# A decoder step on one core: the first tile of the out projection is multiplied in another order, and the last normalization is spread in pieces over three engines and two DMA queues

## The chip, the cores and the metric

The kernel runs on one core of one Trainium2 chip. The metric is the device time of one execution in microseconds. One execution has been profiled; its span runs from the first to the last instruction.

## The reference, cut to what matters

The reference is one inference step of a small hybrid decoder over 544 tokens: a prompt of 512 and 8 samples of 4. The first layer is a state space mixer, the second attends over dilated windows, and a final norm ends the trunk:

```
u = rmsnorm(h, g_norm) @ w_in                       # 1024 -> 5152: z, x|B|C, dt
...                                                 # convolution, SSD scan -> y (l, 2048)
y = rmsnorm(y * silu(z), g_gate)                    # z: the last column tiles of w_in to be computed
h = h + y @ w_out                                   # "out projection", 2048 -> 1024
...                                                 # shared K/V, dilated window attention
h = h + y_att @ b_w_out                             # 1024 -> 1024
y_out = h * rsqrt(mean(h * h) + eps) * final_norm   # over the 1024 features of a token
```

All arrays are float32.

## The kernel before, in words

Features lie on the 128 partitions and tokens in the free dimension. A projection is computed in tiles of 128 output features. For each there are two PSUM buffers: `pa` for the first 256 tokens and `pb` for the other 288. Three PSUM buffers of this kind take turns.

Every product is made of three fast ones. A weight is split into a high part (`whi`, rounded, by ScalarE, L199) and a low part (`wlo`, the remainder, by VectorE, L200), an activation likewise. Per slice of 128 input features TensorE multiplies high by high, high by low and low by high (`proj_steps`, called through `full`). `load_w` fetches a weight of eight slices into one of three `wraw` buffers, on SyncE's DMA queue, and splits it; `whi` and `wlo` have two buffers each.

The first stage ends with ten tiles of z (`z_tile` in `filler_a`). Their order is a list, and each weight is fetched and split while the tile ahead of it is multiplied. The gated result `v` (four groups of four slices) is split by `v_split` into `vh` and `vl` (L757 on ScalarE, L758 on VectorE): groups 0 and 1 within the z tiles, 2 and 3 behind them. The sum of squares `ssq` is collected on GpSimd (L598).

The out projection has 16 input slices, so each of its tiles has two weights: slices 0 to 7 and 8 to 15 (`load_out`). In the first tile, `m == 0`, the slices are multiplied in an order of their own: 0 to 11 into `pa`, 0 to 11 into `pb`, 12 to 14 into both, the mean square `ms` of the gated result, then slice 15. The later tiles go straight through.

The kernel is recorded in a framework that schedules it: the order of the instructions on each engine comes from the program's order, from priorities (`high_priority` around the splits) and from what each instruction waits for. Matmuls of the second layer and of its out projection (`out_proj`) are made in a fixed order.

At the end `out_proj` adds the last product to the residual for two parts of the tokens, 272 each. Part 0 is normalized while part 1 is multiplied. For part 1 everything behind the last product is in the open: `norm_sum` (the squares summed over features, into PSUM `ms`), `rstd_fin` (ScalarE's square root, VectorE's reciprocal, L267, three scalings of an identity into `dgs`, L270, and one product with ones that spreads the factors over all partitions, `rp` in PSUM), then `norm_mul` with four multiplies on VectorE (L1456), two feature tiles at a time, each followed by a DMA to the output on SyncE's queue (L1457). `dgs`, `tmps` and `accs` are pieces of one SBUF tile `e`, and appear as `e` in the rows.

Of the kernel before, what the change touches and what calls it, by code (L numbers as in the profile page):

```python
# [12 lines left out]
F32 = mybir.dt.float32  # L13
F32R = mybir.dt.float32r
AF = mybir.ActivationFunctionType
ALU = mybir.AluOpType
# [7 lines left out]
T = SEQ + NB * TS  # L24
HA = 256
HB = T - HA
KD = D // 128
# [97 lines left out]
def tile_yoco_step(  # L125
# [6 lines left out]
    nc = tc.nc  # L132
    dma = nc.sync.dma_start
    pinned = [False]

    def pin(ins):
        if pinned[0]:
            tc.keep_in_program_order(ins)
# [3 lines left out]
    def mm(*a, **k):  # L142
        pin(nc.tensor.matmul(*a, **k))  # L143
# [4 lines left out]
    const = ctx.enter_context(tc.tile_pool(name="const", bufs=1))  # L148
# [8 lines left out]
    def pj(name, cols=512):  # L157
        return psum.tile([128, cols], F32, name=name, tag="pj", bufs=3)

    def pss(name, shape=(128, 512)):  # L160
        return psum.tile(list(shape), F32, name=name, tag="ss", bufs=5)
# [10 lines left out]
    ident = const.tile([128, 128], F32, name="ident")  # L172
    make_identity(nc, ident)
    ones = const.tile([128, 128], F32, name="ones")
# [5 lines left out]
    epst = const.tile([128, 1], F32, name="epst")  # L180
# [7 lines left out]
    def fetch_w(src):  # L188
        raw = wpool.tile([128, 8, 128], F32, name="wraw", bufs=3)
        dma(raw, src)  # L190
        return raw

    def split_w(raw, both=None, lo_eng=nc.vector, fixed=False):
        if both is None:
            hi = wpool.tile([128, 8, 128], F32R, name="whi", bufs=2)
            lo = wpool.tile([128, 8, 128], F32R, name="wlo", bufs=2)
        else:
            hi, lo = both[:, 0], both[:, 1]
        a = nc.scalar.activation(hi, raw, AF.Copy)  # L199
        b = lo_eng.tensor_tensor(lo, raw, f32(hi), op=ALU.subtract)  # L200
        if fixed:
            hold(a)
            hold(b)
        return hi, lo

    def load_w(src, both=None, lo_eng=nc.vector):
        raw = fetch_w(src)
        with tc.high_priority():
            return split_w(raw, both, lo_eng)
# [10 lines left out]
    def proj_steps(p, ws, act_h, act_l, c0, c1, k0=0, k1=None, order=None):  # L220
        n = len(ws) * 8
        o = p[:, 0:c1 - c0]
        order = order or range(n)
        for i in range(k0, n if k1 is None else k1):
            k = order[i]
            hi, lo = ws[k // 8]
            ah, al = act_h[k // 4][:, k % 4, c0:c1], act_l[k // 4][:, k % 4, c0:c1]
            mm(o, hi[:, k % 8, :], ah, start=i == 0, stop=False)
            yield
            mm(o, hi[:, k % 8, :], al, start=False, stop=False)  # L230
            yield
            mm(o, lo[:, k % 8, :], ah, start=False, stop=i == n - 1)
            yield

    def full(*a, **k):
        for _ in proj_steps(*a, **k):
            pass
# [147 lines left out]
    for i in range(2):  # L385
        sq, xa = sqx[i][:, :, 0:HA], x_t[i][:, :, 0:HA]
        n = 4 - 2 * i
# [6 lines left out]
    hi = wpool.tile([128, 8, 128], F32R, name="whi", bufs=2)  # L394
    lo = wpool.tile([128, 8, 128], F32R, name="wlo", bufs=2)
# [34 lines left out]
    for i in range(3):  # L430
        cbs.append(conv_in(first[i], pp[i]))
        pb = pj("pb")
# [7 lines left out]
    dgs = tm[:, 1200:1584].rearrange("p (a b) -> p a b", b=128)  # L440
# [312 lines left out]
    def v_split(g, i):  # L753
        gg = g_gate[:, 4 * g + i:4 * g + i + 1]
        if i == 0:
            v_h[g], v_l[g] = half("vh", F32R), half("vl", F32R)
        nc.scalar.activation(v_h[g][:, i, :], v_t[g][:, i, :], AF.Copy, scale=gg)  # L757
        nc.vector.scalar_tensor_tensor(v_l[g][:, i, :], v_t[g][:, i, :], gg, f32(v_h[g][:, i, :]),  # L758
                                       op0=ALU.mult, op1=ALU.subtract)

    v_h, v_l = [None] * 4, [None] * 4

    def filler_a():
        nxt = load_w(w_in[5])
        for i, (kind, t) in enumerate(IN_ORDER):
            if i < 5:
                continue
            w = nxt
            if i + 1 < len(IN_ORDER):
                nxt = load_w(w_in[i + 1])  # L770
            yield from (conv_tile if kind == "x" else z_tile)(t, w)
            if kind == "x" and t == 3:
                yield from tok_transposes()
            if kind == "z" and t in (13, 14):
                for j in range(4):
                    v_split(t - 13, j)
# [12 lines left out]
    for c0, c1 in ((0, HA), (HA, T)):  # L789
        for i in range(2):  # L790
            p = pj("pa")
# [34 lines left out]
    ms = pss("ms")  # L826
# [35 lines left out]
        (nc.gpsimd if m < KD - 1 else nc.vector).tensor_tensor(hss, hss, sq, op=ALU.add)  # L862

    def load_out(m):
        return [load_w(w_out[m, :, 0:8, :]), load_w(w_out[m, :, 8:16, :])]

    def bias_tables():
        rl = wk.tile([66, 384], F32, name="rl", tag="tv", bufs=2)
# [53 lines left out]
    for m in range(KD):  # L922
        w = nxt
        pa, pb = pj("pa"), pj("pb")
        if m == 0:
            full(pa, w, v_h, v_l, 0, HA, 0, 12)
            full(pb, w, v_h, v_l, HA, T, 0, 12)
            full(pa, w, v_h, v_l, 0, HA, 12, 15)
            full(pb, w, v_h, v_l, HA, T, 12, 15)
            ms_add(ms, ssq, inv_i, True, True)  # L930
            full(pa, w, v_h, v_l, 0, HA, 15)
            full(pb, w, v_h, v_l, HA, T, 15)
            nxt = load_out(1)
            prev = pa, pb
            continue
        if m == 1:
            full(pa, w, v_h, v_l, 0, HA, 0, 5)
            rs_v = rstd_of(ms)
            h1_tile(0, *prev)
            full(pa, w, v_h, v_l, 0, HA, 5)  # L940
        else:
            full(pa, w, v_h, v_l, 0, HA)
        if m + 1 < KD:
            nxt = load_out(m + 1)
        full(pb, w, v_h, v_l, HA, T)
        h1_tile(m, pa, pb)
        next(tables, 0)
# [30 lines left out]
    for i, (f, h, wi) in enumerate(order):  # L978
        w = [nxt]
        pa, pb = pj("pa"), pj("pb")  # L980
        if i == 0:
# [4 lines left out]
            ms = pss("ms")  # L986
# [35 lines left out]
    for k in range(4):  # L1022
        b1, b2 = (wk.tile([128, T], F32, name="hb", bufs=2) for _ in range(2))
# [33 lines left out]
    scale = 1.0 / math.sqrt(128.0)  # L1057
# [370 lines left out]
    def out_proj():  # L1428
        h2 = [half("h2"), half("h2")]
        for i in range(2):  # L1430
            dma(h2[i], h1d[:, 4 * i:4 * i + 4, :])
        e = half("e").rearrange("p a b -> p (a b)")
        accs, tmps = [e[:, HB * i:HB * i + HB] for i in range(2)], [e[:, HB * (2 + i):HB * (3 + i)] for i in range(2)]
        dgs = [e[:, HB * (4 + i):HB * (5 + i)] for i in range(2)]
        wos = {}

        def get(m):
            if m < KD and m not in wos:
                wos[m] = load_w(wo[m], half("wo", F32R, (128, 2, 8, 128)) if m < KD - 2 else None)

        def norm_sum(part, c0, c1):
            n = c1 - c0
            b0s = (0, 128, n - 128) if n > 256 else (0, 128)
            ms = pss("ms")
            for s_ in (0, 1):
                for b, b0 in enumerate(b0s):
                    mm(ms[:, b:b + 1], (accs, tmps)[s_][part if s_ == 0 else 1][:, b0:b0 + 128], inv_d,
                       start=s_ == 0 and b == 0, stop=s_ == 1, skip_group_check=True)
            return ms, n, b0s

        def norm_mul(sums, part, c0, c1):
            ms, n, b0s = sums
            rs = rstd_fin(ms, n, b0s, dgs[part])
            for m in range(0, KD, 2):
                hm = h2[m // 4][:, m % 4:m % 4 + 2, c0:c1]
                nc.vector.tensor_tensor(hm, hm, rs[:, None, 0:n].to_broadcast([128, 2, n]), op=ALU.mult)  # L1456
                dma(yT[:, m:m + 2, c0:c1], hm)  # L1457

        get(0)
        parts = ((TH, T), (0, TH))  # L1460
        for part, (c0, c1) in enumerate(parts):
            n = c1 - c0
            acc = accs[part]
            for m in range(KD):
                get(m + 1)
                p = pj("pa")
                yield from proj_steps(p, [wos[m]], y_h, y_l, c0, c1, order=(0, 1, 2, 3, 5, 7, 6, 4))
                if part and m == 0:
                    sums = norm_sum(0, *parts[0])
                if part and m == 1:  # L1470
                    norm_mul(sums, 0, *parts[0])
                hm = h2[m // 4][:, m % 4, c0:c1]
                sq = acc if m == 0 else tmps[m % 2]
                nc.vector.tensor_tensor(hm, p[:, 0:n], hm, op=ALU.add)
                nc.scalar.activation(sq[:, 0:n], hm, AF.Square)
                if 0 < m < KD - 1:
                    nc.gpsimd.tensor_tensor(acc[:, 0:n], acc[:, 0:n], sq[:, 0:n], op=ALU.add)
                nc.scalar.activation(hm, hm, AF.Copy, scale=g_f[:, m:m + 1])
        norm_mul(norm_sum(1, *parts[1]), 1, *parts[1])

    ahead = [0]

# [129 lines left out]
```

## Time and profile before

| | |
|---|---|
| three runs | 945.29 us median, 944.85 to 950.9 |
| profiled execution | 946.21 us |
| its span | 944.4 us, 21805 instructions |
| TensorE busy | 916.7 us, 97% |
| VectorE, ScalarE, GpSimd busy | 682.1, 478.7, 200.5 us |
| mean granted TensorE clock | 0.991 |

PE is TensorE's matmuls, PEld its weight loads, DVE is VectorE, ACT ScalarE, POOL GpSimd, and SPq and ACTq are the DMA issues of SyncE and ScalarE. A row of the order of time gives the start, the length, the engine, the line, the operation, what is written from what, and in square brackets the idle time ahead of it with what ended it. A product of two plain float32 tiles, such as `ms`, `rp` or `idle`, is two matmul records. A row of the waits gives the total, the number and the longest. A row of a stretch gives its length, then the busy time and the instructions of PE, PEld, DVE, ACT and POOL, the granted clock, the DMA share and GB/s.

### The profile page before, as it was taken

How to read it: one execution, taken by the hardware profiler on the slowest of the kernel's cores; microseconds unless marked ns; L12 is line 12 of the kernel's file. 1: busy time of each engine (PE TensorE's matmuls, PEld its weight loads, DVE VectorE, ACT ScalarE, POOL GpSimd, SP SyncE). 2: the span in 40 equal slices, each digit the busy share in tenths (PEclk: the TensorE clock that was granted, in tenths of full speed). 3: DMA queues.
4: the chain of work that ended last, by engine and by line, in shares of the span. 5: the costliest groups of instructions: out<-in, count | busy, mean ns of one | idle time of the engine just before them, and what ended most of it. 6: DMA issues, size and time to landing. Idle time of an engine off the chain costs nothing.

```text
span 944.4 us, 21805 instructions
## 1 busy us (share of the span) xinstructions
PE 916.7 (97%) x8645; PEld 844.0 (89%) x8645; DVE 682.1 (72%) x1423; ACT 478.7 (51%) x1069; POOL 200.5 (21%) x295
## 2 busy tenths in 40 slices
PE   7999999899999998999999999999999999999996
PEld 5999888789788888999999999988888988888996
DVE  6688988997997889544589435876677766778632
ACT  5558744655556644322245213555555555557642
POOL 2232644733725642111101000000000000000021
PEclk9999999899999999999999999999999999999998
DMA  7252255254454452436377555757767767785411
GB/s 261 87 141 92 101 198 189 81 201 142 157 179 154 167 177 100 147 102 216 102 240 233 178 191 197 267 174 263 247 201 259 272 203 259 262 249 192 158 44 52
DMA packets 75934, 168.49 MB, mean 178 GB/s; under 512 B 19446, under 2 KB 37192, under 8 KB 75320
## 3 DMA queue, kind: packets, MB, share of 16 engines
q1 hardware_dynamic: 71880, 154.91, 50.1%
q10 hardware_dynamic: 2880, 9.44, 2.6%
q0 software_dynamic: 1072, 2.74, 1.1%
q8 instruction: 68, 1.11, 0.5%
q14 instruction: 34, 0.28, 0.1%
HBM read 141.14 MB, written 25.93 MB: 177 GB/s over the span
## 4 chain that ended last, share of the span: by engine, by line
PE 85%; DVE 6%; DMA 5%; ACT 2%; POOL 1%; issue 1%; DVEq 0%; SPq 0%; ACTq 0%
PE pa L143 34%; PE pb L143 29%; PE sp L143 3%; PE pv L143 2%; PE so L143 2%; PE s L143 2%; DMA m<-aed 2%; DMA kc<-ck 1%; PE yd L143 1%; PE csp L143 1%; PE w L146 1%; PE ptp L146 1%; PE yo L143 1%; PE xp L146 1%; PE yos L143 1%
## 5 line engine op out<-in xcount | busy, mean ns | idle before, releaser
L199 ACT ACTIVATE whi<-wraw 128x1024 fp32r<-128x1024 f32 x72 | 76.1, 1057 | 99.2 <-PE pb L143 64.7
L200 DVE TENSOR_TENSOR wlo<-wraw,whi 128x1024 fp32r<-128x1024 f32 x71 | 88.8, 1251 | 51.6 <-ACT whi L199 51.3
L143 PE MATMUL pa<-bq,whi 128*128 128x272 f32 x512 | 103.1, 296 | 0.0
L143 PE MATMUL pa<-xh,whi 128*128 128x256 f32 (+1 forms) x320 | 92.7, 293 | 3.3 <-ACT xh L365 3.3
L143 PE MATMUL pb<-xh,whi 128*128 128x288 f32 (+1 forms) x304 | 90.4, 299 | 3.9 <-ACT cb L331 3.9
L143 PE MATMUL pb<-xl,whi 128*128 128x288 f32 (+1 forms) x304 | 91.3, 302 | 0.9 <-DVE xl L368 0.8
L143 PE MATMUL pa<-xl,whi 128*128 128x256 f32 (+1 forms) x320 | 90.8, 287 | 0.9 <-DVE xl L368 0.8
L143 PE MATMUL pb<-xh,wlo 128*128 128x288 f32 (+1 forms) x304 | 87.4, 299 | 0.0
L143 PE MATMUL pa<-xh,wlo 128*128 128x256 f32 (+1 forms) x320 | 85.0, 283 | 0.0
L143 PEld LDWEIGHTS pa<-bq,whi 128*128 128x128 f32 x512 | 81.2, 189 | 0.9
L143 PE MATMUL pb<-bq,whi 128*128 128x272 f32 x384 | 77.2, 296 | 0.5 <-DVE kv L1103 0.5
L143 PE MATMUL pa<-bq,wlo 128*128 128x272 f32 x256 | 74.1, 290 | 0.0
L529 DVE SCALAR_TENSOR_TENSOR co<-cb,cvp,co 128x568 f32<-128x568 f32 x72 | 66.3, 921 | 1.2 <-ACT co L527 0.2
L143 PEld LDWEIGHTS pa<-xh,whi 128*128 128x128 f32 x320 | 60.7, 190 | 6.2 <-ACT xh L365 3.7
L143 PEld LDWEIGHTS pa<-xl,whi 128*128 128x128 f32 x320 | 60.7, 190 | 3.4 <-DVE xl L368 1.4
L143 PEld LDWEIGHTS pb<-xl,whi 128*128 128x128 f32 x304 | 57.8, 190 | 6.5 <-issue 4.4
L143 PEld LDWEIGHTS pb<-xh,whi 128*128 128x128 f32 x304 | 58.0, 191 | 5.0 <-ACT cb L331 4.1
L143 PEld LDWEIGHTS pb<-bq,whi 128*128 128x128 f32 x384 | 60.8, 189 | 1.8 <-DVE kv L1103 0.8
L1339 POOL COPY lse<-mxs 128x1 f32<-128x1 f32 x16 | 4.6, 289 | 267.7 <-DVE mxs L1337 267.7
L143 PEld LDWEIGHTS pa<-xh,wlo 128*128 128x128 f32 x320 | 58.0, 188 | 1.2 <-issue 0.9
L1162 ACT ACTIVATE whi<-wraw 128x512 fp32r<-128x512 f32 x64 | 40.1, 627 | 37.1 <-PE pa L143 17.5
L143 PEld LDWEIGHTS pb<-xh,wlo 128*128 128x128 f32 x304 | 56.6, 190 | 2.2 <-issue 2.2
(379 smaller groups left out, 2771.4 us busy)
## 6 DMA issues: line engine op xcount, KB each, us to landing
wraw<-w_in SPq DMA_DIRECT2D x40, 512.0 KB
kc<-ck SPq DMA_DIRECT2D x32, 640.0 KB
vc<-cv SPq DMA_DIRECT2D x32, 640.0 KB
wraw<-wb SPq DMA_DIRECT2D x32, 512.0 KB
s<-s SPq DMA_DIRECT2D x16, 512.0 KB
m<-aed SPq DMA_DIRECT2D x16, 512.0 KB
ssmS<-s ACTq DMA_DIRECT2D x16, 512.0 KB
wraw<-w_out SPq DMA_DIRECT2D x16, 512.0 KB
```

What stands on the lines that cost most here:

```text
L143: pin(nc.tensor.matmul(*a, **k))
L146: pin(nc.tensor.transpose(*a))
L199: a = nc.scalar.activation(hi, raw, AF.Copy)
L200: b = lo_eng.tensor_tensor(lo, raw, f32(hi), op=ALU.subtract)
L529: nc.vector.scalar_tensor_tensor(o, cb[:, k:k + n], cvp[:, ti, k:k + 1], o, op0=ALU.mult, op1=ALU.add)
L1162: nc.scalar.activation(hi, src[p][j], AF.Copy)
L1339: nc.gpsimd.tensor_copy(lse[:, i16:i16 + 1], mx[:, 2:3])
```

## The change

The first weight of the out projection is fetched and split by the last round of `filler_a` (before: by `load_out`, called behind it). In the tile `m == 0` slices 0 to 7 go into `pa` and then into `pb`, in each with all products of the high weight ahead of those of the low one; slices 8 to 11 follow for both.

The end gets a function of its own, `norm_last`. The scalings of the identity are shared between ScalarE (its middle piece) and VectorE. Six products of ones by ones stand ahead of the spread, and their result is not used. The spread is made in two pieces, 128 and 144 wide. ScalarE copies it to SBUF. GpSimd multiplies the last two feature tiles with the copy, and ScalarE's queue writes them; VectorE multiplies the other six from PSUM, and SyncE's queue writes these.

```
+    out_first = []
...
+            else:
+                out_first.append(load_w(w_out[0, :, 0:8, :]))
...
-        return [load_w(w_out[m, :, 0:8, :]), load_w(w_out[m, :, 8:16, :])]
+        return [load_w(w_out[m, :, 0:8, :]) if m else out_first[0], load_w(w_out[m, :, 8:16, :])]
...
         if m == 0:
-            full(pa, w, v_h, v_l, 0, HA, 0, 12)
-            full(pb, w, v_h, v_l, HA, T, 0, 12)
+            for p, c0, c1 in ((pa, 0, HA), (pb, HA, T)):
+                hi, lo = w[0]
+                for k in range(8):
+                    mm(p[:, 0:c1 - c0], hi[:, k, :], v_h[k // 4][:, k % 4, c0:c1], start=k == 0, stop=False)
+                    mm(p[:, 0:c1 - c0], hi[:, k, :], v_l[k // 4][:, k % 4, c0:c1], start=False, stop=False)
+                for k in range(8):
+                    mm(p[:, 0:c1 - c0], lo[:, k, :], v_h[k // 4][:, k % 4, c0:c1], start=False, stop=False)
+            full(pa, w, v_h, v_l, 0, HA, 8, 12)
+            full(pb, w, v_h, v_l, HA, T, 8, 12)
...
+        def norm_last(sums, part, c0, c1):
+            ms, n, b0s = sums
+            sd = const.tile([128, 5], F32, name="sd", bufs=2)
+            nc.scalar.activation(sd[:, 0:3], ms[:, 0:3], AF.Sqrt, bias=epst)
+            nc.vector.reciprocal(sd[:, 0:3], sd[:, 0:3])
+            idle = pss("idle")
+            for _ in range(6):
+                mm(idle[:, 0:128], ones, ones, start=True, stop=True)
+            dg, rp = dgs[part], pss("rp")
+            nc.scalar.activation(dg[:, 128:256], ident, AF.Copy, scale=sd[:, 1:2])
+            nc.vector.tensor_scalar(dg[:, 0:128], ident, sd[:, 0:1], None, op0=ALU.mult)
+            nc.vector.tensor_scalar(dg[:, 256:n], ident[:, 384 - n:128], sd[:, 2:3], None, op0=ALU.mult)
+            for b0, b1 in ((0, 128), (128, n)):
+                mm(rp[:, b0:b1], ones, dg[:, b0:b1], start=True, stop=True, skip_group_check=True)
+            rs = tmps[0][:, 0:n]
+            nc.scalar.copy(rs, rp[:, 0:n])
+            for m in range(KD - 2, KD):
+                hm = h2[m // 4][:, m % 4, c0:c1]
+                nc.gpsimd.tensor_tensor(hm, hm, rs, op=ALU.mult)
+                nc.scalar.dma_start(yT[:, m, c0:c1], hm)
+            for m in range(0, KD - 2, 2):
+                hm = h2[m // 4][:, m % 4:m % 4 + 2, c0:c1]
+                nc.vector.tensor_tensor(hm, hm, rp[:, None, 0:n].to_broadcast([128, 2, n]), op=ALU.mult)
+                dma(yT[:, m:m + 2, c0:c1], hm)
...
-        norm_mul(norm_sum(1, *parts[1]), 1, *parts[1])
+        norm_last(norm_sum(1, *parts[1]), 1, *parts[1])
```

What this does to the order on the engines is seen at three places. The first is VectorE at the change from the z tiles to the out projection: `pa` and `pb` are those of the last z tiles, the first `L200` splits slices 0 to 7 of the out projection's first weight, the second slices 8 to 15. Before:

```order
L592 TENSOR_TENSOR v<-v,uz 128x544
L200 TENSOR_TENSOR wlo<-wraw,whi 128x1024
L565 SCALAR_TENSOR_TENSOR uz<-zth,pb 128x288
L592 TENSOR_TENSOR v<-v,uz 128x544
L565 SCALAR_TENSOR_TENSOR uz<-zth,pa 128x256
L592 TENSOR_TENSOR v<-v,uz 128x544
L758 SCALAR_TENSOR_TENSOR vl<-v,gn,vh 128x544 x4
L200 TENSOR_TENSOR wlo<-wraw,whi 128x1024
L565 SCALAR_TENSOR_TENSOR uz<-zth,pb 128x288
```

After the change VectorE has the same rows in the same order here, and so have ScalarE, GpSimd and SyncE.

The second place is TensorE in the first tile of the out projection, where slice 7 ends and what follows begins. Before, the first and second weight half follow each other in `pa`, and `pb` comes behind slice 11:

```order
L143 MATMUL pa<-vh,whi 128x256
L143 MATMUL pa<-vl,whi 128x256
L143 MATMUL pa<-vh,wlo 128x256
L143 MATMUL pa<-vh,whi 128x256
L143 MATMUL pa<-vl,whi 128x256
L143 MATMUL pa<-vh,wlo 128x256
L143 MATMUL pb<-vh,whi 128x288
L143 MATMUL pb<-vl,whi 128x288
```

After, from slice 7 of `pa` to slice 0 of `pb`, and then, behind the dots, from slice 7 of `pb` to slice 8 of `pa`:

```order
L143 MATMUL pa<-vl,whi 128x256
L143 MATMUL pa<-vh,wlo 128x256 x8
L143 MATMUL pb<-vh,whi 128x288
L143 MATMUL pb<-vl,whi 128x288
...
L143 MATMUL pb<-vl,whi 128x288
L143 MATMUL pb<-vh,wlo 128x288 x8
L143 MATMUL pa<-vh,whi 128x256
L143 MATMUL pa<-vl,whi 128x256
L143 MATMUL pa<-vh,wlo 128x256
```

So 24 matmuls into `pb` have moved in between slices 7 and 8 of `pa`.

The third place is the end of the program, with what each instruction waits for. VectorE before:

```order
L270 TENSOR_SCALAR e<-ident,sd 128x128
L270 TENSOR_SCALAR e<-ident,sd 128x16
L1456 TENSOR_TENSOR h_11459<-h_11459,rp 128x2x272 [waits PE_49]
L1456 TENSOR_TENSOR h_11459<-h_11459,rp 128x2x272
L1456 TENSOR_TENSOR h_11460<-h_11460,rp 128x2x272 x2
```

VectorE after, then ScalarE after and TensorE after:

```order
L1481 TENSOR_SCALAR e<-ident,sd 128x128 [waits DVE_49]
L1482 TENSOR_SCALAR e<-ident,sd 128x16
L1493 TENSOR_TENSOR h_11459<-h_11459,rp 128x2x272 [waits Activation_49]
L1493 TENSOR_TENSOR h_11459<-h_11459,rp 128x2x272
L1493 TENSOR_TENSOR h_11460<-h_11460,rp 128x2x272
```

```order
L1515 ACTIVATE h_11460<-h_11460,gn 128x272 [waits Activation_49]
L1474 ACTIVATE sd<-ms,epst 128x3 [waits PE_49]
L1480 ACTIVATE e<-ident,sd 128x128 [waits DVE_49]
L1486 COPY e<-rp 128x272 [waits PE_49,Pool_49]
L1490 DMA yT<-h_11460 128x272 [waits Pool_49] x2
```

```order
L143 MATMUL ms<-inv,e 128x1 x2
L143 MATMUL idle<-ones 128x128 [waits PE_49]
L143 MATMUL idle<-ones 128x128 x5
L143 MATMUL rp<-e,ones 128x128 [waits DVE_49]
L143 MATMUL rp<-e,ones 128x144 [waits DVE_49,Activation_49]
```

VectorE's first multiply, which waited for TensorE, now waits for ScalarE, and the count that it waits for is that of the copy L1486. The spread stands behind the idle products in TensorE's queue.

## The prediction

> **What bounds the kernel now.** I read the page first, then the waits of the matrix engine, then the order of time around the two places that the change touches.
>
> ```profile
> PE 916.7 (97%) x8645; PEld 844.0 (89%) x8645; DVE 682.1 (72%) x1423; ACT 478.7 (51%) x1069; POOL 200.5 (21%) x295
> PE 85%; DVE 6%; DMA 5%; ACT 2%; POOL 1%; issue 1%; DVEq 0%; SPq 0%; ACTq 0%
> ```
>
> TensorE is busy for 916.7 of the span's 944.4 us and carries 85% of the chain that ended last. So an edit is worth something only where it removes a wait of TensorE or shortens the stretch behind its last matmul. There are 27.7 us of idle TensorE in all. The view of its waits says what ended them:
>
> ```profile
> PE pb L143 <- ACT cb L331: 3.9, 1, 3.9
> PE pa L143 <- ACT xh L365: 3.3, 1, 3.3
> PE pa L143 <- DVE wlo L200: 2.9, 1, 2.9
> PE s L143 <- DMA kc<-ck: 0.6, 2, 0.4
> ```
>
> The first two lie in the prologue, which the change leaves alone. The third is one wait of 2.9 us for the low part of a weight. The order of time puts it in the first tile of the out projection (TensorE, then VectorE):
>
> ```profile
> 369.85 0.28 PE L143 MATMUL pa<-vh,whi 128*128 128x256 f32 x1
> 372.80 0.28 PE L143 MATMUL pa<-vl,whi 128*128 128x256 f32 x1
> 375.93 0.38 PE L143 MATMUL pa<-vh,wlo 128*128 128x256 f32 x1 [2.86 <-DVE wlo L200]
> 376.15 0.28 PE L143 MATMUL pa<-vh,whi 128*128 128x256 f32 x1
> 377.22 0.29 PE L143 MATMUL pb<-vh,whi 128*128 128x288 f32 x1
> 382.02 0.28 PE L143 MATMUL pa<-vh,whi 128*128 128x256 f32 x1
> 365.46 1.22 DVE L200 TENSOR_TENSOR wlo<-wraw,whi 128x1024 fp32r<-128x1024 f32 x1
> 367.59 0.41 DVE L565 SCALAR_TENSOR_TENSOR uz<-zth,pa 128x256 f32<-128x256 f32 x1
> 368.56 6.18 DVE L758 SCALAR_TENSOR_TENSOR vl<-v,gn,vh 128x544 fp32r<-128x544 f32 x4
> 374.66 1.21 DVE L200 TENSOR_TENSOR wlo<-wraw,whi 128x1024 fp32r<-128x1024 f32 x1
> 376.16 0.77 DVE L758 SCALAR_TENSOR_TENSOR vl<-v,gn,vh 128x544 fp32r<-128x544 f32 x1
> 377.49 3.28 DVE L758 SCALAR_TENSOR_TENSOR vl<-v,gn,vh 128x544 fp32r<-128x544 f32 x3
> ```
>
> Slices 0 to 7 (first weight half) are 24 matmuls into pa, 369.85 to about 372.7. Slice 8 begins with the high part, and the matmul with the low part, due at 372.92, starts at 375.93. Note which weight is late. The split at 365.46 is that of the **first** half, done at 366.7, over 3 us before its use. The one at 374.66 is that of the **second** half. It stands in VectorE's queue behind the four splits of v that start at 368.56, and ends at 375.87.
>
> **The change at the out projection.** The words promise an earlier split. But VectorE's rows are the same before and after (the order shown above), and so are ScalarE's and SyncE's here: the split of the first half already stood in the last z tile. This edit by itself I cost at 0. Placing the low-part matmuls of a half behind its high ones gains nothing either, since that low part was ready at 366.7.
>
> What does count is that the first half is now multiplied into **both** pa and pb before the second half is touched. Pace in pa: 25 matmuls from 369.85 to 372.80, 0.118 each. Pace in pb: 36 from 377.22 to 382.02, 0.133 each. After the change: 24 into pa until 372.70, 24 into pb (3.20) until 375.90, two of slice 8, then its low part at 376.13. That weight is ready at 375.93, so the wait is gone, by a margin of 0.20. The new first wait of pb is for its buffer, last read by VectorE at 367.59 to 368.00: no cost.
>
> The number of matmuls is unchanged, so what is saved is the shift: 375.93 against the 372.92 at which that matmul was due, 3.01, and the 0.10 by which the restart exceeds the pace (0.22 from 375.93 to 376.15). Slice 12 starts at 378.92 in place of 382.02: **3.1 us**.
>
> What is late next? Slices 12 to 14 need the splits of v at 376.16 (done 376.93) and the first two of 377.49 (done by about 379), used at about 379.0, 379.4 and 379.7; the order of waits is one split per slice. The mean square needs GpSimd's last sum:
>
> ```profile
> 378.47 1.72 POOL L598 TENSOR_TENSOR ssq<-ssq,sq 128x544 f32<-128x544 f32 x1 [5.01 <-ACT sq L597]
> ```
>
> It ends at 380.19 and is now used at 381.2. Slice 15 follows the mean square, behind the last split (380.77). Nothing of this binds. Behind it TensorE has no gap that could swallow the gain:
>
> ```profile
> 386.00:480.00 94.00, 94.00 (x741) 93.27 (x740) 48.51 (x74) 27.41 (x34) 11.35 (x12) 1.00 0.47 147
> 480.00:565.00 85.00, 85.00 (x669) 83.84 (x669) 55.75 (x108) 32.85 (x71) 5.04 (x10) 1.00 0.65 215
> 565.00:700.00 135.00, 134.80 (x1508) 122.42 (x1507) 93.93 (x256) 66.05 (x164) 2.90 (x10) 1.00 0.69 227
> 700.00:845.00 145.00, 144.64 (x1870) 126.79 (x1868) 102.76 (x311) 79.17 (x214) 2.47 (x9) 1.00 0.75 245
> ```
>
> The first number behind the length is TensorE's busy time: 458.4 of 459 us. So I carry all of the 3.1 to the end. Its bounds are 0 (all given back) and 3.2 (the margin as well).
>
> **The change at the end.** The stretch behind the last product, then the output DMA by the microsecond (DMA share and GB/s stand last):
>
> ```profile
> 935.18 0.83 PE L143 MATMUL ms<-inv,e 128*128 128x1 f32 x6 [0.49 <-ACT e L1475]
> 936.04 0.26 ACT L266 ACTIVATE sd<-ms,epst 128x3 f32<-128x3 f32 x1 [0.36 <-PE ms L143]
> 936.34 0.17 DVE L267 RECIPROCAL sd<-sd 128x3 f32<-128x3 f32 x1 [1.74 <-ACT sd L266]
> 936.55 0.63 DVE L270 TENSOR_SCALAR e<-ident,sd 128x128 f32<-128x128 f32 x3
> 937.32 0.70 PE L143 MATMUL rp<-e,ones 128*128 128x272 f32 x2 [1.32 <-DVE e L270]
> 938.05 2.61 DVE L1456 TENSOR_TENSOR h<-h,rp 128x544 f32<-128x544 f32 x4 [0.88 <-PE rp L143]
> 938.85 2.25 SPq L1457 DMA_DIRECT2D yT<-h  x4
> 939.00:940.00 1.00, 0.00 (x0) 0.00 (x0) 1.00 (x3) 0.00 (x0) 0.00 (x0) 0.50 0.24 86
> 940.00:941.00 1.00, 0.00 (x0) 0.00 (x0) 0.67 (x2) 0.00 (x0) 0.00 (x0) 0.50 1.04 349
> 941.00:942.00 1.00, 0.00 (x0) 0.00 (x0) 0.00 (x0) 0.00 (x0) 0.00 (x0) 0.50 1.06 369
> 942.00:943.00 1.00, 0.00 (x0) 0.00 (x0) 0.00 (x0) 0.00 (x0) 0.00 (x0) 0.50 0.88 310
> ```
>
> The DMA engines begin at 939.76 (0.24 of that microsecond) and are full until 942.88, some 3.1 us for 1.11 MB; the span ends 1.5 us later. So the drain, and not VectorE's four multiplies, sets the end: only the time of the **first** write counts. I work that out.
>
> Six idle products are queued between the mean square and the spread, 12 records like those of yo, eight of which take 0.99:
>
> ```profile
> 337.01 1.05 PE L143 MATMUL yo<-CT,st 128*128 128x128 f32 x8
> 338.00 1.09 PE L143 MATMUL yd<-m,xdt 128*64 128x128 f32 x16
> ```
>
> That is 0.124 each. The six records of ms from 935.18 at that pace let them start at 935.93, and they hold TensorE until 937.42. Behind them wait the pieces of the spread, though their inputs are there by 937.0: one 128-wide scaling on VectorE and one on ScalarE side by side, each about 0.28, replace three in a row, a saving hidden entirely by the idle products. The two pieces are four records: 937.42 to about 938.08, against 938.02 before: +0.06.
>
> Then ScalarE copies the spread row to SBUF for GpSimd. In the order VectorE's first multiply no longer waits for TensorE but for ScalarE, so it is behind that copy. A 128x272 copy out of PSUM doesn't stand in the trace; the nearest row is
>
> ```profile
> L564 ACT ACTIVATE zth<-pb x14: 384/392/412, 133.0 to 370.9; 128x288 f32<-128x288 f32 x14
> ```
>
> so 0.39, plus 0.03 and 0.04 for the two hand-overs (as from ms to sd, and sd to the reciprocal): VectorE starts at 938.54 in place of 938.05, **+0.49**. The first write leaves as much later, and the drain follows.
>
> [...]
>
> GpSimd's two multiplies: from 938.65, 0.78 each by its sum of this size in the rows below, done about 940.2; the writes on ScalarE's queue have started by 941.2, well ahead of the drain's end at about 943.4. VectorE isn't slowed beside GpSimd in this form:
>
> ```profile
> 916.03 2.61 DVE L1456 TENSOR_TENSOR h<-h,rp 128x544 f32<-128x544 f32 x4
> 916.55 0.78 POOL L1477 TENSOR_TENSOR e<-e 128x272 f32<-128x272 f32 x1 [9.49 <-ACT e L1475]
> ```
>
> Taking a quarter of the multiplies off VectorE is worth 0, since the drain covers it.
>
> [...]
>
> **Sum.** -3.1 + 0.5 = **-2.6 us**. The profiled execution took 946.21 (span 944.4 and 1.81 around it), so 943.6 on its scale. The median of the runs, 945.29, is 0.92 lower: **942.7 us**, -0.28%. A measurement of this kernel can't tell less than about 1% (9.5 us) from no change.
>
> **Rivals** (on the median's scale).
> *The own queue pays.* A quarter of the bytes leaves beside the rest, the drain falls from 3.1 to 2.3: -3.1 + 0.5 - 0.8, 941.9 us. Against it: the full DMA engines. Chance 0.08.
> *The idle products run slowly.* The same form at the program's start takes 0.23 a record:
>
> ```profile
> 1.06 4.63 PE L143 MATMUL wps<-ones 128*128 128x128 f32 x20 [1.06 <-DVE epst L181]
> ```
>
> Twelve take 2.8 in place of 1.5 and the four of the spread 0.4 more: tail about +2.1, 944.2 us. Against it: ms runs at 0.124 a record just before. Chance 0.09.
> *The change doesn't do what it says.* The split isn't earlier, so if VectorE's 374.66 slips by more than the margin of 0.20, or a v split of slices 12 to 15 does, part of the wait returns. With half of it: 944.2 us. Chance 0.08.
> *The gain is given back, and the end's cost stays:* slower. The place is attention, 565 to 845, at DMA shares of 0.69 and 0.75: if the loads of kc there were paced by the DMA engines and not by buffers that TensorE frees, TensorE would reach them 3.1 early and wait 3.1 more. It decides from 2.6 us of added waits on; the price is the tail alone, 945.8 us. For it: the two waits on kc (0.6). Against: nothing else there waits. Chance 0.08.
>
> The forecast as summed has 0.67. From the rivals at both ends and half a microsecond of scatter I take 941.0 to 946.0. All cases lie within 1%: same 0.97, faster 0.01, slower 0.02 for what I haven't seen.
>
> **What would show it.** Right: no wait of TensorE on wlo at the out projection, slice 12 near 378.9, and the stretch from the last product to the end of the span 0.5 longer, with idle products up to about 937.4 - 3.1 = 934.3 and VectorE's multiplies behind the copy. Wrong: a wait on wlo or vl left over; PE waits on kc that grow; a first write ahead of the old one; or a drain shorter than 3.1.

## The result: 0.9949 of the time before, and the profile after

The change took the median from 947.58 us (13 runs of the kernel before) to **942.89 us** (13 runs, 941.12 to 946.2), a ratio of **0.9949 [0.9935, 0.9964]**. That is 4.8 us (3.4 to 6.2), half a per cent. The interval leaves out 1, but the whole of it lies within the 1% that the prediction counts as the same time. One of the twelve executions of `small_first` below took 1765.66 us and is left out of its ratio. The profiled execution took 942.13 us, with a span of 940.4 us, 4.0 less than before.

The page of the kernel after, first the busy time by engine, then the engines' shares of the chain that ended last:

```profile
PE 917.3 (98%) x8659; PEld 846.0 (90%) x8659; DVE 682.7 (73%) x1421; ACT 479.3 (51%) x1071; POOL 203.3 (22%) x297
PE 91%; DVE 4%; DMA 2%; ACT 1%; POOL 1%; issue 0%; DVEq 0%; ACTq 0%; SPq 0%
```

TensorE is busy 0.6 us more (14 records: 12 of idle products and two of the spread) in a span that is 4.0 shorter. Its largest waits (us in total, times, longest):

```profile
PE pb L143 <- ACT cb L331: 3.9, 1, 3.9
PE pa L143 <- ACT xh L365: 3.3, 1, 3.3
PE yos L143 <- DMA s<-s: 2.5, 1, 2.5
```

The two waits of the prologue are where they were, and the third of before, 2.9 us on the low part of the out weight, is gone. The order of time shows what stands in its place:

```profile
369.56 0.28 PE L143 MATMUL pa<-vh,whi 128*128 128x256 f32 x1
371.44 1.11 PE L143 MATMUL pa<-vh,wlo 128*128 128x256 f32 x8
372.39 0.29 PE L143 MATMUL pb<-vh,whi 128*128 128x288 f32 x1
374.40 1.21 DVE L200 TENSOR_TENSOR wlo<-wraw,whi 128x1024 fp32r<-128x1024 f32 x1
374.52 1.23 PE L143 MATMUL pb<-vh,wlo 128*128 128x288 f32 x8
375.82 0.28 PE L143 MATMUL pa<-vh,wlo 128*128 128x256 f32 x1
378.61 0.28 PE L143 MATMUL pa<-vh,whi 128*128 128x256 f32 x1
380.87 1.17 PE L143 MATMUL ms<-inv,ssq 128*128 128x1 f32 x10
```

VectorE finishes the split of the second half at 375.61, as late as before. But TensorE works on `pb` until then and needs it at 375.82, 0.21 later. From the first product of `vh` to the mean square (the stretch called "the first out tile" below) it is now 11.31 us; before it was 14.43 (369.85 to 384.28). Behind it nothing waits that did not wait before; the sum of the four stretches from 386 to 845:

```profile
sum 459.00, PE 458.62 PEld 427.16 DVE 302.38 ACT 205.94 POOL 19.61; mean PE 114.66 PEld 106.79 DVE 75.60 ACT 51.48 POOL 4.90
```

TensorE is busy for 458.6 of 459 us, against 458.4 before. The end, in order of time:

```profile
930.86 0.83 PE L143 MATMUL ms<-inv,e 128*128 128x1 f32 x6 [0.49 <-ACT e L1512]
931.55 1.58 PE L143 MATMUL idle<-ones 128*128 128x128 f32 x12
932.23 0.40 ACT L1480 ACTIVATE e<-ident,sd 128x128 f32<-128x128 f32 x1 [0.24 <-DVE sd L1475]
932.97 0.63 PE L143 MATMUL rp<-e,ones 128*128 128x128 f32 x4
933.69 0.39 ACT L1486 COPY e<-rp 128x272 f32<-128x272 f32 x1 [1.06 <-PE rp L143]
934.11 1.98 DVE L1493 TENSOR_TENSOR h<-h,rp 128x544 f32<-128x544 f32 x3 [1.45 <-ACT e L1486]
934.16 1.48 POOL L1489 TENSOR_TENSOR h<-h,e 128x272 f32<-128x272 f32 x2 [5.46 <-ACT e L1486]
934.86 1.67 SPq L1494 DMA_DIRECT2D yT<-h  x3
```

And by the microsecond (the granted clock, DMA share and GB/s stand last):

```profile
935.00:936.00 1.00, 0.00 (x0) 0.00 (x0) 1.00 (x2) 0.00 (x0) 0.63 (x1) 1.00 0.23 83
936.00:937.00 1.00, 0.00 (x0) 0.00 (x0) 0.09 (x1) 0.00 (x0) 0.00 (x0) 1.00 1.04 354
937.00:938.00 1.00, 0.00 (x0) 0.00 (x0) 0.00 (x0) 0.00 (x0) 0.00 (x0) 0.79 1.04 362
938.00:939.00 1.00, 0.00 (x0) 0.00 (x0) 0.00 (x0) 0.00 (x0) 0.00 (x0) 0.50 0.90 316
```

VectorE's first multiply waits for ScalarE's copy. It starts 3.25 us behind the second-half mean square (930.86) where it was 2.87 before (935.18 to 938.05). The drain is full and 3.1 us long, as before. From that mean square to the end of the span it is 9.50 us (930.86 to 940.36), against 9.23 (935.18 to 944.41). The profile's 4.0 us split up as 3.11 in the first out tile, 0.29 ahead of it, 0.91 in attention, and 0.27 lost behind it.

### The profile page after: what moved, and what is told of

Same layout as the page of the kernel before. It is cut to its first block, busy times and chain, and to the rows that moved or that the text cites. A ratio compares the mean times of both kernels' runs of the same rounds, so it can differ in the third digit from the quotient of the medians.

```text
span 940.4 us, 21836 instructions
## 1 busy us (share of the span) xinstructions
PE 917.3 (98%) x8659; PEld 846.0 (90%) x8659; DVE 682.7 (73%) x1421; ACT 479.3 (51%) x1071; POOL 203.3 (22%) x297
## 3 DMA queue, kind: packets, MB, share of 16 engines
q0 software_dynamic: 1072, 2.74, 1.1%
## 4 chain that ended last, share of the span: by engine, by line
PE 91%; DVE 4%; DMA 2%; ACT 1%; POOL 1%; issue 0%; DVEq 0%; ACTq 0%; SPq 0%
PE pa L143 36%; PE pb L143 31%; PE sp L143 3%; PE so L143 3%; PE pv L143 2%; PE s L143 2%; PE yd L143 2%; PE csp L143 1%; PE yo L143 1%; PE xp L146 1%; PE ptp L146 1%; PE w L146 1%; PE yos L143 1%; PE up L143 1%; POOL v L592 1%; DMA kc<-ck 1%
## 5 line engine op out<-in xcount | busy, mean ns | idle before, releaser
L200 DVE TENSOR_TENSOR wlo<-wraw,whi 128x1024 fp32r<-128x1024 f32 x71 | 89.2, 1256 | 47.0 <-ACT whi L199 46.6
```

## The experiments

**The two halves of the change, apart.** Each was timed beside the kernel before.

`proj_only` keeps the old end:

```
-        norm_last(norm_sum(1, *parts[1]), 1, *parts[1])
+        norm_mul(norm_sum(1, *parts[1]), 1, *parts[1])
```

> The out projection's edit alone, with the end of before. My theory: TensorE's wait on the low part is gone, so the first out tile (first product with vh to the mean square) takes 11.3 us instead of 14.4; the stretch from the second half of the final mean square to the end of the span is 9.2 us as before. All of the change's gain is here: 3.1 us off before in sum, ratio about 0.9967, and 0.3 us below the changed kernel. Rival: the shift also makes the stages behind it shorter (attention was 0.9 shorter in the profile of the changed kernel): then the ratio is below 0.996 and attention is shorter here too.

Measured: 943.63 us, **0.9946 [0.9923, 0.9969]**; first out tile 11.32 us.

`end_only` keeps the old out projection and has `norm_last`:

```
-        norm_mul(norm_sum(1, *parts[1]), 1, *parts[1])
+        norm_last(norm_sum(1, *parts[1]), 1, *parts[1])
```

> The end's edit alone, with the out projection of before. My theory: the wait of 2.9 us on wlo is there, the first out tile takes 14.4 us, and the stretch from the second half of the final mean square to the end takes 9.5 us instead of 9.2: no gain, 0.3 us slower, ratio 1.0003, not to be told from 1. Rival (the pieces, GpSimd and the own queue pay): a stretch under 9.2 us and a ratio below 0.999. If attention is shorter here than before as well, its length has nothing to do with the projection.

Measured: 947.91 us, **1.0001 [0.998, 1.0022]**; its stretch at the end is 9.52 us (934.15 to 943.67), and the wait on the low part is back with 2.9 us. So all that can be measured comes from the out projection, and the end costs 0.3 us against the profile of before, which no timing here resolves.

**The out projection, split again.** `columns_only` has only the new order of the columns, with the three products of a slice side by side and the weight split where it was:

```
-            full(pa, w, v_h, v_l, 0, HA, 0, 12)
-            full(pb, w, v_h, v_l, HA, T, 0, 12)
+            full(pa, w, v_h, v_l, 0, HA, 0, 8)
+            full(pb, w, v_h, v_l, HA, T, 0, 8)
+            full(pa, w, v_h, v_l, 0, HA, 8, 12)
+            full(pb, w, v_h, v_l, HA, T, 8, 12)
```

> Before with one edit: in the first out tile slices 0 to 7 go into pa and then into pb, ahead of slices 8 to 11, each slice with its three products in the old order; no earlier load, no high part first. My theory: this is the whole of the gain: the first out tile takes 11.3 us, no wait on wlo, ratio as for the projection's edit alone, about 0.9967. Rival (the early split or the high part first matters): a wait of over 0.5 us on wlo is left.

Measured: 942.84 us, **0.995 [0.9931, 0.9969]**; first out tile 11.30 us, no wait on the low part.

`high_first_only` has the rest of it, the split moved ahead and the low products behind the high ones, in the old order of the columns:

```
+            hi, lo = w[0]
+            for p, c0, c1 in ((pa, 0, HA), (pb, HA, T)):
+                ...  # the eight high slices, then the eight low ones, as in the change
+                full(p, w, v_h, v_l, c0, c1, 8, 12)
```

> The early load and the high part first, as the change's words have it, but the columns in the old order: slices 0 to 11 into pa, then into pb; the end of before. My theory: nothing gained, TensorE still waits 2.9 us on the low part of slices 8 to 15, the first out tile takes 14.4 us, ratio 1.000. Rival: the early split is what removes the wait: no wait, 11.3 us, ratio 0.9967.

Measured: 948.59 us, **0.9999 [0.9979, 1.0018]**; TensorE waits 2.8 us on the low part, and the first out tile takes 14.41 us. The whole effect is the order of the columns. The earlier split and the high part ahead of the low, which the change's own words put first, are worth nothing that these runs can show: the interval is 0.2% to either side of 1, and the tile took 14.41 us against 14.43.

**What the wait really costs.** The ratios with the new order lie around 0.995, 4.7 us, while the trace shows 3.1. The profile of `end_only` held a clue. Its TensorE has the old order and the old wait, but look at the pace behind it:

```profile
374.60 0.58 PE L143 MATMUL pa<-vh,wlo 128*128 128x256 f32 x1 [2.88 <-DVE wlo L200]
374.98 0.41 PE L143 MATMUL pa<-vh,whi 128*128 128x256 f32 x1
375.19 0.41 PE L143 MATMUL pa<-vl,whi 128*128 128x256 f32 x1
375.41 0.41 PE L143 MATMUL pa<-vh,wlo 128*128 128x256 f32 x1
```

The products start 0.21 us apart, not 0.118, and the tile takes 15.70 us. Three more profiles of the kernel before, unchanged, were to tell whether that belonged to one execution:

> The kernel before, unchanged, profiled once more. In two profiles with the old column order the granted TensorE clock stays at 1.00 behind the wait on the second half's low part and the first out tile takes 14.4 us; in the third (end_only) the clock falls to 0.50 from about 374.6 to 377.4, the matmuls there take 0.21 instead of 0.118, and the tile takes 15.7. Theory A (a gap of 2.9 us brings the clock down in a share of the executions, so the change also removes up to 1.3 us of slow matmuls): in some of three more looks the tile takes 15.5 to 15.8 and the clock reads 0.5 behind the gap, in the others 14.4 and 1.00. Rival B (the slow stretch belonged to end_only's code or was a single event): 14.4 and 1.00 in all three.

> A third profile of the kernel before, unchanged; the expectations are those of the second: 15.5 to 15.8 us for the first out tile with a clock of 0.5 behind the gap (theory A, in a share of the looks), or 14.4 and 1.00 (rival B, always).

> A fourth profile of the kernel before, unchanged; the expectations are those of the second: 15.5 to 15.8 us for the first out tile with a clock of 0.5 behind the gap (theory A, in a share of the looks), or 14.4 and 1.00 (rival B, always).

It did not. The first of them, in order of time:

```profile
374.55 0.39 PE L143 MATMUL pa<-vh,wlo 128*128 128x256 f32 x1 [2.86 <-DVE wlo L200]
374.77 0.28 PE L143 MATMUL pa<-vh,whi 128*128 128x256 f32 x1
376.18 0.44 PE L143 MATMUL pb<-vh,wlo 128*128 128x288 f32 x1
376.42 0.44 PE L143 MATMUL pb<-vh,whi 128*128 128x288 f32 x1
384.42 1.17 PE L143 MATMUL ms<-inv,ssq 128*128 128x1 f32 x10
```

And by the microsecond (the granted clock is the third number from the end):

```profile
375.00:376.00 1.00, 1.00 (x11) 1.00 (x10) 1.00 (x2) 0.00 (x0) 0.00 (x0) 1.00 0.22 70
376.00:377.00 1.00, 1.00 (x7) 1.00 (x6) 1.00 (x3) 0.71 (x2) 0.00 (x0) 0.51 0.93 303
377.00:378.00 1.00, 1.00 (x6) 1.00 (x5) 0.97 (x2) 0.58 (x1) 0.91 (x1) 0.50 0.38 152
378.00:379.00 1.00, 1.00 (x6) 1.00 (x5) 1.00 (x1) 0.00 (x0) 0.80 (x1) 0.50 0.00 0
379.00:380.00 1.00, 1.00 (x8) 1.00 (x7) 0.38 (x1) 0.00 (x0) 0.00 (x0) 0.79 0.00 0
```

The wait ends at 374.55 and TensorE runs at full pace for 1.5 us. Then the granted clock drops to 0.50 and stays there for 3.4 us (what is missing to 1.00 in the last four rows adds up to 1.70, at half clock 3.4 us); the products of `pb` stand 0.24 apart, not 0.133. All profiles of the old order, and those of the new one, by the same reading (the last column is explained below):

| kernel | first out tile, us | at half clock, us | most of the wait in one clock step, us |
|---|---|---|---|
| before | 14.43 | 0 | 1.88 |
| `high_first_only` | 14.41 | 0 | 1.49 |
| `end_only` | 15.70 | 3.4 | 2.29 |
| `before_look2` | 15.96 | 3.4 | 1.94 |
| `before_look3` | 15.97 | 3.4 | 2.12 |
| `before_look4` | 15.54 | 3.4 | 2.25 |
| new order (after and the six others with it) | 11.30 to 11.32 | 0 | no wait |

The old order has a mean of 15.34 us (six profiles), 4.0 above the new. The wait of 2.6 to 2.9 us is always there; in four of six executions it also brings the clock down, which costs another 1.1 to 1.5 us. That is theory A, and rival B falls. The moment of the fall is not the same in all four: it is 1.5 us behind the wait's end here and 0.6 us ahead of it in `end_only` (374.01 against 374.60).

The traces show what sets the two executions without a fall apart. The points at which the granted clock changes lie a multiple of 3.41 us apart: in the first profile they are 13.13, 16.55, 166.74, 173.56 and 938.15, which is 1, 44, 2 and 224 such steps, and in the profile after 12.58, 15.99, 166.18, 173.00, 248.09, 251.51 and 937.59, which is 1, 44, 2, 22, 1 and 201. In every profile the steps are counted from such a change (in `high_first_only`, where the clock stayed up behind the wait, back from 937.60). The wait falls across two steps, and the last column of the table has the larger part. Two of these steps, the first profile's and then that of `before_look2` (PE's busy time stands behind the length):

```profile
371.54:374.95 3.41, 1.53 (x14) 1.33 (x12) 3.41 (x4) 1.01 (x2) 1.84 (x2) 1.00 0.00 0
372.61:376.02 3.41, 1.47 (x12) 1.47 (x13) 3.41 (x6) 0.00 (x0) 0.00 (x0) 1.00 0.08 23
```

Where 1.94 us or more of the wait lay in one step, the clock was at half from the end of that step on; where it was 1.88 or less, the clock stayed. So among waits of about this length the place on the steps goes with the fall, without an exception. No run moved the wait on purpose, so this is read and not tested, and it is read for this wait alone: in the profile after, among smaller products, the clock fell at 248.09 behind a step with 1.87 us idle. As an estimate from these numbers, a wait of 2.86 us stays below 1.9 in both steps for 0.95 of every 3.41 us of its position, so that the clock would fall in about 72% of executions; it fell in four of six.

`wait_longer` stretches the gap in the old order:

```
+        for _ in range(again):    # 2 for the second half of the first out weight, otherwise 0
+            lo_eng.tensor_tensor(lo, raw, f32(hi), op=ALU.subtract)
         b = lo_eng.tensor_tensor(lo, raw, f32(hi), op=ALU.subtract)
```

> The kernel before, with the low part of the second half of the first out weight computed three times in a row (same result), which holds VectorE 2 x 1.21 us longer. TensorE's wait on it grows from 2.9 to 5.3 us. If the gap's length alone made the clock fall (theory A, with a longer gap as a surer cause), the granted clock reads 0.5 behind it and the first out tile takes 14.4 + 2.4 + 1.3 to 2 = 18.1 to 18.8 us. If the clock doesn't depend on the gap (rival B), it stays at 1.00 and the tile takes 14.4 + 2.4 = 16.8.

Its wait and the products behind it:

```profile
378.87 0.58 PE L143 MATMUL pa<-vh,wlo 128*128 128x256 f32 x1 [6.16 <-DVE wlo L202]
379.25 0.41 PE L143 MATMUL pa<-vh,whi 128*128 128x256 f32 x1
388.48 1.17 PE L143 MATMUL ms<-inv,ssq 128*128 128x1 f32 x10
```

And its granted clock (third number from the end), in steps of 2 us:

```profile
374.00:376.00 2.00, 0.00 (x0) 0.00 (x0) 2.00 (x4) 0.00 (x0) 0.00 (x0) 0.72 0.00 0
376.00:378.00 2.00, 0.00 (x0) 0.00 (x0) 2.00 (x3) 0.23 (x1) 0.00 (x0) 0.50 0.00 0
378.00:380.00 2.00, 1.13 (x5) 1.13 (x6) 2.00 (x2) 1.07 (x2) 1.43 (x1) 0.50 0.10 12
380.00:382.00 2.00, 2.00 (x12) 2.00 (x12) 2.00 (x4) 0.00 (x0) 0.02 (x1) 0.57 0.67 248
```

The gap is 6.16 us, not 5.3: in VectorE's order two operations on `uz` and `v` stood in between the three splits. By that gap the tile would take 14.4 + 3.3 = 17.7 us at full clock. It took 18.98, and the clock was at 0.50 for 6.8 us (2 x 1.71 missing to 1.00, at half clock), twice as long as behind the short gap; 4.0 of the 6.8 passed within the gap (374.88 to 378.87). The steps fit: 2.16 us of the gap lie in the one that ends at 374.88, the next is idle throughout, the third holds 0.58, and the clock was at half for the two steps up to 381.71. Theory A holds again; this run lasted 951.62 us.

**The end, edit by edit.** Four kernels vary `norm_last` with everything else as after. All lengths run from the second-half mean square.

| kernel | first multiply of VectorE | end of the span |
|---|---|---|
| before | 2.87 | 9.23 |
| after | 3.25 | 9.50 |
| `no_idle` | 3.03 | 9.28 |
| `own_bank` | 2.78 | 9.14 |
| `no_idle_own_bank` | 2.98 | 9.34 |
| `small_first` | 3.09 | 9.46 |

`no_idle` leaves out the six idle products:

```
-            for _ in range(6):
-                mm(idle[:, 0:128], ones, ones, start=True, stop=True)
```

> The changed kernel without the six idle products. My theory: they only hold TensorE: the spread starts 0.4 us earlier behind the mean square, at full pace (records 0.12 to 0.16 apart), and the stretch from the second half of the final mean square to the end of the span goes from 9.54 to about 9.1 us. Rival (they keep TensorE at speed): the spread's four records take over 0.9 us instead of 0.63, and the stretch stays at 9.5.

Measured: 945.99 us in one execution; the multiply is 0.22 earlier, since the pieces of the spread no longer stand behind the idle products. The end gains the same 0.22, half of the 0.4 that was expected; the four records of the spread take 0.71 us, so the rival falls here.

`own_bank` computes the spread row once more, whole, in a buffer of its own for ScalarE's copy:

```
+            rq = pss("rq")
+            mm(rq[:, 0:n], ones, dg[:, 0:n], start=True, stop=True)
-            nc.scalar.copy(rs, rp[:, 0:n])
+            nc.scalar.copy(rs, rq[:, 0:n])
```

> The changed kernel with one product more: the spread goes once more into a second PSUM bank, and ScalarE copies that one, so that VectorE reads the first bank alone and waits for TensorE. My theory: VectorE's first multiply starts 0.4 us earlier, so does the first write, and the stretch from the second half of the final mean square to the end is about 9.15 us. Rival (the drain or GpSimd's late tiles set the end): 9.5 as in the changed kernel, though VectorE starts earlier.

Measured: 944.93 us in one execution. The rows of its end:

```profile
934.01 0.83 PE L143 MATMUL ms<-inv,e 128*128 128x1 f32 x6 [0.49 <-ACT e L1514]
936.12 0.63 PE L143 MATMUL rp<-e,ones 128*128 128x128 f32 x4
936.79 1.98 DVE L1495 TENSOR_TENSOR h<-h,rp 128x544 f32<-128x544 f32 x3 [0.98 <-PE rp L143]
937.30 0.39 ACT L1488 COPY e<-rq 128x272 f32<-128x272 f32 x1 [1.52 <-PE rq L143]
```

VectorE waits for TensorE again and starts 0.47 earlier than after. The end comes 0.36 earlier, as expected. So the shared buffer was the whole cost of the new end, and without it the end stands 0.09 ahead of the old one (9.14 against 9.23), in one profile.

`no_idle_own_bank` has both edits.

> Both: no idle products and the second bank. My theory: the two terms add, 0.4 and 0.4 off 9.54: about 8.7 us, half a microsecond under before. Rival (GpSimd's tiles, fed by the copy of the second bank, are late now): no lower than 9.1, with GpSimd's writes landing last.

Measured: 947.98 us in one execution; the end takes 9.34, not 8.7, so the two gains did not add up. In this execution the clock fell at 938.79, 0.12 us into the spread: its four records take 1.14 us, not 0.63. The rival's sign is there too, since ScalarE's queue, with GpSimd's tiles, issues until 943.10 and SyncE's until 942.25. But the DMA engines show no gap (0.47 in the microsecond from 941, in which they begin, then 1.05, 1.03 and 0.65), so these tiles did not hold up the drain. `small_first` has both edits and also multiplies and writes its first two tiles one by one:

```
-            for m in range(0, KD - 2, 2):
+            for m0, m1 in ((0, 1), (1, 2), (2, 4), (4, 6)):
```

> As the one with no idle products and the second bank, and VectorE's first two multiplies take one feature tile each, so that the first write can leave after 0.4 us of multiplying instead of 0.7. My theory (the drain is full from the first write on): 0.3 us less again, about 8.4 us from the second half of the final mean square to the end, 0.8 under before; with the out projection's 3.1 some 3.9 us under before, ratio about 0.996, not to be told from the changed kernel's. Rival: the drain has gaps now, and the stretch stays at 8.7.

Measured: 943.52 us, **0.9959 [0.9943, 0.9976]**, not better than after, and an end of 9.46 where about 8.4 was expected. Its end, in order of time:

```profile
933.40 0.83 PE L143 MATMUL ms<-inv,e 128*128 128x1 f32 x6 [0.49 <-ACT e L1512]
935.21 1.25 PE L143 MATMUL rp<-e,ones 128*128 128x128 f32 x4 [0.97 <-DVE e L1479]
936.49 2.05 DVE L1493 TENSOR_TENSOR h<-h,rp 128x272 f32<-128x272 f32 x4 [1.28 <-PE rp L143]
937.00 1.98 SPq L1494 DMA_DIRECT2D yT<-h  x4
```

And three of its microseconds:

```profile
935.00:936.00 1.00, 0.80 (x3) 0.82 (x4) 0.20 (x2) 0.17 (x1) 0.00 (x0) 0.50 0.00 0
937.00:938.00 1.00, 0.36 (x1) 0.00 (x0) 1.00 (x3) 0.39 (x1) 0.09 (x1) 0.50 0.14 50
938.00:939.00 1.00, 0.00 (x0) 0.00 (x0) 0.53 (x1) 0.00 (x0) 1.00 (x2) 0.50 0.78 259
```

The first write leaves 3.60 us behind the mean square, where it was 4.00 after. But the clock is at 0.50 and the spread takes 1.25 us, and the drain now starts ahead of its data: 0.14 and then 0.78 of the engines, where after has 0.23 and then 1.04. So the idle products may not be useless. They cost some 0.2 us, and in the three profiles that have them (after, `end_only`, `own_bank`) the spread always takes 0.63 us. Three are too few to show that the products are the reason. Without them the clock had fallen ahead of the spread, or at its start, in five of eleven: in these two of the three with the new end, and in three of the eight with the old one (`before_look4`, `proj_only`, `wait_longer`), whose two records then take 1.24 to 1.25 us and not 0.70 and whose end takes 9.77 to 9.78 us and not 9.2.

So the old end has a mean of 9.4 us over its eight profiles (five of 9.2, three of 9.8), and the new one of 9.5. No timed version beat the new order of the columns with either end by a margin that could be measured, and three of the four kernels of this part were executed once; by the traces the best end is `own_bank`'s, 9.14 us at full clock.

## Why the prediction was right, point by point, and where it was off

- **The time**: 942.7 us forecast, 942.89 measured, within the range and the class. The level is luck: two misses of over 2 us each cancelled. The sum was −2.6 us and was set under the median of three runs, 945.29; the kernel before has a median of 947.58 over 13. Against that the change is −4.8 [−6.2, −3.4], so the sum fell short by 0.8 to 3.6. The interval of the ratio, 0.15% to either side, also answers the remark that less than about 1% can't be told from no change.
- **The column order**: the mechanism held in every detail: the wait gone, a margin of 0.21 (0.20 forecast), slice 12 at 378.61, which is 9.05 us behind the first product (9.07 forecast). In the profile it is 3.11 us for 3.1. The term that was mis-sized is this one all the same: the way from 369.85 to 382.02 was read from one execution in which the clock had happened to hold. Over six profiles the term is 4.0. "The number of matmuls is unchanged, so what is saved is the shift" left out the matmuls behind the wait, which in four of the six profiles ran at a clock of 0.50 for 3.4 us.
- **The split moved, the high part first**: 0 forecast, 0.9999 measured.
- **The end**: +0.49 forecast, +0.27 in the profile, and +0.1 over the means, since the forecast took the old end's full clock for granted too. The wait of VectorE for ScalarE's copy was sized well: 0.43, and the multiply now starts 0.51 behind the spread's end (933.60) where it started 0.03 behind it; `own_bank` gives 0.47. The other 0.06 had the wrong sign: the spread ended 2.74 behind the mean square, where it was 2.84 before, since the idle products began 0.69 and not 0.75 behind it and took 0.118 and not 0.124 a record (931.55 to 932.97).
- **The own queue and GpSimd's quarter**: 0 forecast. The drain is 3.1 us with DMA shares of 1.04 and 1.04 at 354 and 362 GB/s; before, with one queue, it was 3.1 us with 1.04 and 1.06 at 349 and 369.
- **Idle products at 0.23 us a record**: that rival falls; they ran at 0.118.
- **Given back later**: so does this one. TensorE's waits in attention did not grow. The 0.91 us that the profile gained there are scatter: profiles of the old order have 301.4 to 303.1 us from the first `bq` to the first `yh` product, the new order 301.4 to 303.5.
- **What is still open**: by the means over all profiles the change is worth 4.0 at the out projection and costs 0.1 at the end (9.4 to 9.5 us). That explains 3.9 us, and the ratio's centre of 4.8 is 0.9 away, inside its interval. How often the clock falls is known from a few profiles only, and what decides it is read from seven traces and was not tried by a run.

## What to carry to other kernels

The wait of the engine that bounds this kernel, TensorE, cost its own length (2.6 to 2.9 us) and, in four of six executions, 1.1 to 1.5 us more for a stretch of 3.4 us at a clock of 0.50: price both, and read the clock behind a wait in more than one execution. Here the clock fell where 1.94 us or more of the wait lay in one of its 3.41 us steps. When a weight half is late, give TensorE the other columns of the half that is there, rather than trying to make the late one earlier. When two engines read one PSUM buffer, look at who waits for whom: here a copy of 0.39 us ahead of the critical reader took back more than its pieces had saved.

## What was not expected of the hardware

- The granted clock fell to 0.50 for 3.4 us behind a gap of 2.6 to 2.9 us in four of six executions: in two of them 1.3 and 1.5 us after TensorE had begun to work again, in the other two 0.4 and 0.6 us before. With a gap of 6.2 us it was down for 6.8. The place of the gap among the steps of 3.41 us went with the fall in all seven profiles.
- Behind the last product the clock falls within half a microsecond in one execution (before: 0.57 of full speed in the microsecond from 938, with the last product ending at 938.02) and after 4 us in another (after: 0.79 in that from 937, with the last product ending at 933.60).
- The stage ahead of the out projection takes 368.5 to 374.4 us over the fourteen profiles, and is the largest part of the spread between executions (in the four of the kernel before, 368.5 to 373.3 of spans of 944.4 to 950.1). So one profile against another says little: only stretches with the same work can be compared.
